# A two-layer diffusion trunk on one core: the opening takes the key and value product block by block, and tiles get sizes in multiples of 512 bytes

## The chip, the core and the metric

The kernel runs on one core of a Trainium2 chip. Its engines work side by side, each on a queue of its own that it takes strictly in order: TensorE (PE) multiplies, VectorE (DVE) and ScalarE (ACT) work on elements, GpSimd (POOL) helps, and SyncE (SP) issues most transfers from DRAM. Engines wait for each other by semaphores. The metric is the device time of one execution in microseconds (us), and less is better.

## What is computed

Two layers of a token mixer with 512 latent tokens and 256 context tokens of width 1024. Each layer norms and modulates the tokens, projects them with `w_in`, runs attention, a gated MLP with chunks and a convolution beside each other, merges them by gates, and adds a squared-ReLU MLP.

```python
mod  = (jax.nn.silu(c) @ ada_w[l] + ada_b[l])[:, None, :]
sh1, sc1, g1, sh2, sc2, g2 = jnp.split(mod, 6, axis=-1)
h  = modulate(rms_norm(x,  mix_pre_g[l]), sh1,  sc1)      # 512 latent tokens
hc = modulate(rms_norm(xc, mix_pre_g[l]), shc1, scc1)     # 256 context tokens
p  = h @ w_in[l]
q    = apply_rope(q_heads(p, q_norm_g[l]), cos, sin)
k, v = kv_heads(p[..., K_OFF:GU_OFF], k_norm_g[l])
...
attn = latent_attention(q, jnp.concatenate([kc, k], 1), jnp.concatenate([vc, v], 1))
y = mixer_merge(p, attn, ...)       # attention, gMLP and convolution branches, gates, w_out
x = x + g1 * rms_norm(y, mix_post_g[l])
x = x + g2 * rms_norm(sq_relu_mlp(modulate(rms_norm(x, ffn_pre_g[l]), sh2, sc2), w1, w2), ffn_post_g[l])
```

## The kernel before, in words

Products are done in three passes. Each fp32 operand is split into a high and a low part (`whi`, `wlo` for weights, two tiles of `hT`, `hB`, `z` or `gin` for data), and PE multiplies high by high, high by low and low by high. A weight arrives by a transfer of 512 KB into a raw tile (`wraw`, two buffers, and `xraw`, as many as a stage asks for); ScalarE casts it to `whi` (L171), and VectorE or GpSimd subtracts to get `wlo` (L174).

A layer runs through stages: attention, gMLP with the convolution (`gmlp_conv`), `conv_out`, and the MLP. Ahead of the first layer stands the stage `start` (L1045 on). It loads X (six blocks of 128 tokens: X0 to X3 latent, X4 and X5 context), norms them, turns them with PE (`transposed`, L403) into columns `xT`, which ScalarE and VectorE copy out of PSUM in turns (L1066, L1068), gets shift and scale of the first layer in four blocks (`ada_shift_scale(j)`, L303 to L324, each from four transfers of 512 KB of `ada_w`), and modulates and splits the columns into `hT` (`modulated`, L1071 on). Block j of shift and scale serves the column tiles 2j and 2j+1. In `ada_shift_scale` PE leaves sums in four bands of partitions; they are copied to `adrow` (L313), turned by four transposes (L316), and added up by VectorE (L318 to L324).

The key and value weights are four raw loads of 512 KB (`wload_kv`, here kv0 to kv3). The product itself is in `attention` (`keys_values`, L532): 8 column tiles, 6 token blocks, 3 passes, so 144 matmuls of 512 columns, in three PSUM tiles of two banks each (`ps`, three buffers). Other PSUM tiles are single banks (`pq`, two buffers).

In `conv_out`, `across` (L955 on) spreads a value per token over all partitions: for each block of 128 tokens VectorE puts the values on a diagonal (`dg`), and PE multiplies it with a constant (L961); the result is copied to `bc` (L963), with which the eight `yr` tiles are scaled (L1006), activated (L1007) and split into `z` for the product with `w_conv_o`.

No order is written out by hand. The program is put into queues by a scheduler that models the engines' time and picks instructions by it; what the source fixes is which operations there are, in which tiles and with how many buffers, since an instruction that needs a buffer waits for its last reader.

Of the kernel before, what the change touches and what calls it, by code (L numbers as in the profile page):

```python
# [11 lines left out]
F32 = mybir.dt.float32  # L12
# [28 lines left out]
JOINT_DOWN = [1, 0]  # L41
EPS = 1e-6
# [12 lines left out]
def trunk_kernel(ctx: ExitStack, tc: tile.TileContext, x, c, ctx_in, c_ctx, ada_w, ada_b, mix_pre_g, mix_post_g,  # L55
# [4 lines left out]
    cst = ctx.enter_context(tc.tile_pool(name="cst", bufs=1))  # L60
    outer = ctx.enter_context(tc.tile_pool(name="outer", bufs=1))
# [33 lines left out]

    def o_(shape, tag, bufs, dt=F32):
        return outer.tile(shape, dt, tag=tag, bufs=bufs, name=nm(tag))

    def t_(shape, tag, bufs, dt=F32):
        return stage_pool[0].tile(shape, dt, tag=tag, bufs=bufs, name=nm(tag))  # L100

    ident = cst.tile([P, P], F32, name="ident")
# [8 lines left out]
    for r in range(2):  # L111
        nc.gpsimd.memset(pick[:, r, r:r + 1], 1.0)

# [142 lines left out]
    def parameters():  # L256
        rows = t_([P, 2, P], "rows", 1)
        nc.sync.dma_start(rows[0:96, 1, :], ada_b.rearrange("l (t p) -> (l t) p", p=P))
        yield
        for i, src in enumerate((mix_pre_g, mix_post_g, gmlp_norm_g, conv_b, conv_norm_g, conv_norm_b,  # L260
                                 ffn_pre_g, ffn_post_g)):
            nc.sync.dma_start(rows[16 * i:16 * i + 16, 0, :], src.rearrange("l (t p) -> (l t) p", p=P))
            if i < 6:
                yield
# [4 lines left out]
        nc.tensor.transpose(pv[:, 0:P], rows[:, 0, :], ident)  # L269
        nc.tensor.transpose(pv[:, P:P + 100], rows[0:100, 1, :], ident[:100, :100])  # L270
# [25 lines left out]
    def ada_shift_scale(j):  # L296
# [965 lines left out]
```

## Time and profile before

| | |
|---|---|
| median of 3 runs | 2648.12 us (2647.98 to 2650.31) |
| profiled execution, whole | 2647.3 us |
| its span | 2645.5 us |
| PE busy | 2591.1 us, 98% of the span |
| DVE, ACT, POOL busy | 63%, 41%, 16% |
| PE busy in the first 20 us | 6.31 us |

The span is the stretch that the profile covers, from the first to the last instruction; the profiled execution has 1.8 us around it. Matmuls overlap, so their listed durations (0.39 us for 512 columns) are longer than the distance from one start to the next (0.23 us), and the distance is what counts. An idle stretch is read with what ended it: `<-DMA x` is a transfer that landed, `<-ACT x` a result of ScalarE.

### The profile page before, as it was taken

What the parts mean: (1) busy time and instruction counts of PE and PEld (TensorE: products, weight loads), DVE (VectorE), ACT (ScalarE), POOL (GpSimd) and SP (SyncE); (2) the same over time, 40 slices, a digit from 0 to 9 for tenths busy, and PEclk for the clock granted to TensorE, in tenths of its full rate; (3) what the DMA queues carried; (4) which work ended last, traced back from release to release, by engine and by line L of the source; (5) the groups of instructions that cost most, each with busy time, mean ns of one, the idle gap of its engine ahead of it and who ended that gap; (6) DMA issues with size and microseconds to landing.
All of it is one profiled execution on the core that took longest, in us unless ns stands there. A gap on an engine that the chain in (4) does not pass through costs nothing.

```text
span 2645.5 us, 37736 instructions
## 1 busy us (share of the span) xinstructions
PE 2591.1 (98%) x15133; PEld 2266.0 (86%) x15133; DVE 1658.5 (63%) x2663; ACT 1076.2 (41%) x1848; POOL 435.0 (16%) x310
## 2 busy tenths in 40 slices
PE   7999999999999999999999999999999999999998
PEld 5989988888888899888888899888888888988888
DVE  5746847489864648445564478777679855734436
ACT  4646434344134636322131355554343244633324
POOL 0000015466463200000000000000465510000000
PEclk9999999999999999999999999999999999999999
DMA  7211134233345345243464342112433455533233
GB/s 250 63 43 37 36 107 137 62 99 95 104 130 173 102 165 154 76 130 120 127 199 129 121 151 88 57 41 72 124 108 100 138 159 173 155 112 96 96 101 106
DMA packets 322241, 300.13 MB, mean 113 GB/s; under 512 B 11517, under 2 KB 268817, under 8 KB 322065
## 3 DMA queue, kind: packets, MB, share of 16 engines
q1 hardware_dynamic: 309360, 271.20, 33.2%
q10 hardware_dynamic: 12704, 26.51, 2.8%
q8 instruction: 119, 1.95, 0.3%
q14 instruction: 58, 0.47, 0.1%
HBM read 275.63 MB, written 22.04 MB: 113 GB/s over the span
## 4 chain that ended last, share of the span: by engine, by line
PE 92%; DVE 3%; DMA 2%; ACT 2%; issue 1%; SPq 0%; DVEq 0%; ACTq 0%
PE ps L192 44%; PE ps L494 16%; PE ps L206 9%; PE pq L192 8%; PE pq L206 4%; PE pq L669 3%; PE ps L635 2%; PE ps L658 1%; PE ps L532 1%; DVE wlo L174 1%; ACT whi L171 1%; PE ps L919 1%; PE pq L403 0%; PE ps L574 0%; DMA xraw<-in_ada_w_dram 0%
## 5 line engine op out<-in xcount | busy, mean ns | idle before, releaser
L192 PE MATMUL ps<-hB,whi 128*128 128x512 f32 (+1 forms) x2272 | 591.9, 359 | 5.0 <-DVE ff L1175 2.3
L171 ACT CAST whi<-wraw 128x1024 fp32r<-128x1024 f32 x261 | 273.8, 1050 | 638.8 <-PE ps L192 315.9
L174 POOL TENSOR_TENSOR wlo<-wraw,whi 128x1024 fp32r<-128x1024 f32 x96 | 230.7, 2404 | 1549.2 <-ACT whi L171 1533.5
L192 PEld LDWEIGHTS ps<-hB,whi 128*128 128x128 f32 x2272 | 387.6, 188 | 71.3 <-DVE ff L1175 2.7
L837 DVE SCALAR_TENSOR_TENSOR cy<-G,cw,cy 128x768 f32<-128x768 f32 (+1 forms) x464 | 404.3, 888 | 11.5
L192 PE MATMUL ps<-hB,wlo 128*128 128x512 f32 (+1 forms) x1136 | 371.9, 357 | 0.0
L494 PE MATMUL ps<-whi,hT 128*128 128x512 f32 x1152 | 356.7, 389 | 0.6 <-ACT whi L171 0.6
L174 DVE TENSOR_TENSOR wlo<-wraw,whi 128x1024 fp32r<-128x1024 f32 x165 | 204.7, 1241 | 201.1 <-ACT whi L171 196.8
L192 PE MATMUL ps<-hT,whi 128*128 128x512 f32 (+1 forms) x1408 | 318.7, 344 | 0.6 <-ACT gu L915 0.6
L494 PEld LDWEIGHTS ps<-whi,hT 128*128 128x128 f32 x1152 | 216.2, 188 | 46.4 <-ACT whi L171 1.1
L192 PEld LDWEIGHTS ps<-hT,whi 128*128 128x128 f32 x1408 | 221.1, 189 | 34.3 <-ACT gu L915 1.1
L174 DVE TENSOR_TENSOR wlo<-xraw,whi 128x1024 fp32r<-128x1024 f32 x109 | 133.3, 1223 | 185.0 <-ACT whi L171 184.5
L206 PE MATMUL ps<-whi,hT 128*128 128x256 f32 x1280 | 232.0, 283 | 0.0
L192 PEld LDWEIGHTS ps<-hB,wlo 128*128 128x128 f32 x1136 | 199.4, 188 | 31.6
L494 PE MATMUL ps<-wlo,hT 128*128 128x512 f32 x576 | 224.4, 390 | 0.0
L171 ACT CAST whi<-xraw 128x1024 fp32r<-128x1024 f32 x109 | 114.2, 1049 | 258.9 <-PE ps L494 118.9
L206 PEld LDWEIGHTS ps<-whi,hT 128*128 128x128 f32 x1280 | 199.6, 192 | 0.5 <-issue 0.4
L192 PE MATMUL ps<-hT,wlo 128*128 128x512 f32 x704 | 190.2, 343 | 0.0
L206 PE MATMUL ps<-wlo,hT 128*128 128x256 f32 x640 | 181.2, 284 | 0.6 <-DVE wlo L174 0.6
L343 POOL TENSOR_TENSOR asum<-asum,aprod 128x512 f32<-128x512 f32 x84 | 111.6, 1329 | 105.7 <-ACT aprod L341 63.2
L494 PEld LDWEIGHTS ps<-wlo,hT 128*128 128x128 f32 x576 | 108.1, 188 | 22.6 <-issue 0.4
L192 PEld LDWEIGHTS ps<-hT,wlo 128*128 128x128 f32 x704 | 110.2, 189 | 16.0
(299 smaller groups left out, 4315.1 us busy)
## 6 DMA issues: line engine op xcount, KB each, us to landing
wraw<-in_w_in_dram SPq DMA_DIRECT2D x134, 512.0 KB, 3.7
xraw<-in_w_ff_dram SPq DMA_DIRECT2D x89, 512.0 KB, 3.9
wraw<-in_w_ff_dram SPq DMA_DIRECT2D x63, 512.0 KB, 3.9
xraw<-in_ada_w_dram SPq DMA_DIRECT2D x39, 512.0 KB, 5.2
wraw<-in_ada_w_dram SPq DMA_DIRECT2D x33, 512.0 KB, 4.2
araw<-in_ada_w_dram SPq DMA_DIRECT2D x48, 256.0 KB, 2.9
xraw<-in_w_out_dram SPq DMA_DIRECT2D x18, 512.0 KB, 8.3
wraw<-in_w_attn_o_dram SPq DMA_DIRECT2D x16, 512.0 KB, 3.5
```

The costliest lines, as they stand in the source:

```text
L171: nc.scalar.copy(hi, raw)
L174: e.tensor_tensor(lo, raw, hi.bitcast(F32), ALU.subtract)
L192: nc.tensor.matmul(ps[:, d0:d0 + n], wt[:, k, c0:c0 + P], xt[:, s0:s0 + n], start=k == 0 and j == 0, stop=k == nk - 1 and j == 2)
L206: nc.tensor.matmul(o, xt[:, tok0:tok0 + P], wt, start=k == 0 and j == 0, stop=k == nk - 1 and j == 2)
L343: nc.gpsimd.tensor_tensor(sums[r], sums[r], t, ALU.add)
L494: nc.tensor.matmul(o, xt[:, tok], wt[:, k, :], start=kt == k == j == 0, stop=kt == 3 and k == 1 and j == 2)
L532: nc.tensor.matmul(o, xt[:, tok], wt, start=k == 0 and j == 0, stop=k == KB - 1 and j == 2)
L635: nc.tensor.matmul(ps[:, s0 - key0:s0 - key0 + n], a[:, i * P:(i + 1) * P], b[:, s0:s0 + n], start=m == 0, stop=m == 2)
L658: nc.tensor.transpose(pt[:, kt * P:(kt + 1) * P], Pm[:, kt * P:(kt + 1) * P], ident)
L669: nc.tensor.matmul(po[:, :256], a[:, kt0 + kt, vs], b[:, kt, :], start=kt == 0 and m == 0, stop=kt == nkt - 1 and m == 2)
L837: nc.vector.scalar_tensor_tensor(done if t == TAPS - 1 else y, G[:, :, t:t + 256], cw[:, t * 8 + cidx:t * 8 + cidx + 1], y, op0=ALU.mult, ...
L919: nc.tensor.matmul(ps[:, n * P:(n + 1) * P], gv[cidx // 4][:, n, (cidx % 4) * P:(cidx % 4 + 1) * P], wsT[:, g, :], start=True, stop=True)
```

## The change

**The opening.** The key and value product moves from `attention` into the stage `start`, into the function `kv_step` (L1110). For each block j its four column-tile halves are multiplied as soon as they are modulated, latent tokens first and context tokens behind them, and between them stand the passes of the next block of shift and scale. `pe()` keeps these PE instructions in the order of the program; the other engines' queues are still put together by the scheduler. The raw key and value loads get `xraw` tiles of their own (10 instead of 6). X0 to X3 are loaded first, then ada 0, ten small rows, kv0, X4 and X5, and then ada j and kv j in turns. The row `ada_b` is issued by ScalarE. Norms are taken for pairs of blocks, the context transposes go through single banks. In `ada_shift_scale` the four transposes become four matmuls with `every`, a constant of two columns that adds the bands, and VectorE has two operations instead of five.

**Memory.** `tile_in` pads every tile of at least 512 bytes a partition to a multiple of 512; smaller ones go to a pool `tiny` with a filler in front. `dg` goes from one buffer per token block to 2, `junkg` shares the tile `gt`, `gb` shares `rt2`.

On SP this is the queue around the small rows, before and then after. In it X are token blocks, rows are the small parameter rows, and in_w_in loads of 128x2x512 are kv0 and so on.

```order
L262 DMA rows_129<-in_ffn_post_g_dram 16x128
L265 DMA rows_129<-in_q_norm_g_dram 2x128
L266 DMA rows_129<-in_k_norm_g_dram 2x128
L1043 DMA X_104<-in_ctx_dram 128x1024
L1043 DMA X_105<-in_ctx_dram 128x1024
L169 DMA wraw_151<-in_w_in_dram 128x2x512
L169 DMA wraw_157<-in_w_in_dram 128x2x512
L303 DMA xraw_163<-in_ada_w_dram 128x4x256
```

```order
L327 DMA xraw_147<-in_ada_w_dram 128x4x256
L288 DMA rows_135<-in_mix_pre_g_dram 16x128
...
L289 DMA rows_135<-in_q_norm_g_dram 2x128
L290 DMA rows_135<-in_k_norm_g_dram 2x128
L1095 DMA xraw_159<-in_w_in_dram 128x2x512
L1058 DMA X_111<-in_ctx_dram 128x1024
L1058 DMA X_112<-in_ctx_dram 128x1024
L327 DMA xraw_295<-in_ada_w_dram 128x4x256
```

The ten small rows stand together between ada 0 and kv0, where they stood between the X blocks; the context blocks come behind kv0. In both queues an entry waits until the transfer eight places ahead has landed.

On ScalarE this is the queue around the copies of X's columns and the casts `whi` of the key and value weights, before and then after (two pieces: kv0's cast, then kv2's).

```order
L394 ACTIVATE xn_111,ss_262<-X_105 128x1024
L171 CAST whi_153<-wraw_151 128x1024
L171 CAST whi_159<-wraw_157 128x1024
L1068 COPY xT_53_207<-ps_198 128x512
L1068 COPY xT_56_220<-ps_211 128x512
L1068 COPY xT_59_233<-ps_224 128x512
L1068 COPY xT_62_246<-ps_237 128x512
L313 COPY adrow_344<-pq_327 128x512
L171 CAST whi_252<-xraw_250 128x1024
L171 CAST whi_258<-xraw_256 128x1024
```

```order
L207 CAST whi_305<-xraw_159 128x1024
L1082 COPY xT_55_227<-ps_218 128x512
L418 ACTIVATE xn_117,ss_327<-X_111 128x1024
L1082 COPY xT_58_240<-ps_231 128x512
L418 ACTIVATE xn_118,ss_327<-X_112 128x1024
L339 COPY adrow_257<-pq_209 128x512
...
L207 CAST whi_540<-xraw_450 128x1024
L207 CAST hT_119<-xT_87_367 128x256
L1082 COPY xT_93_385<-pq_380 128x256
L207 CAST hT_121<-xT_88_369 128x256
L1082 COPY xT_96_394<-pq_389 128x256
L339 COPY adrow_421<-pq_404 128x512
```

The squares of the context blocks moved behind kv0's cast, between the copies, and kv2's cast came to stand ahead of the last copies of the context columns.

On PE this is `across` in the first layer's `conv_out`, before and then after; hT by whi and wlo is the gate product that runs behind or around it.

```order
L192 MATMUL ps_8390<-hT_126,wlo_8388 128x256
L961 MATMUL ps_8449<-dg_8450,means 128x128
L961 MATMUL ps_8449<-dg_8453,means 128x128
L961 MATMUL ps_8449<-dg_8456,means 128x128
L961 MATMUL ps_8449<-dg_8459,means 128x128
L961 MATMUL ps_8449<-dg_8462,means 128x128
L961 MATMUL ps_8449<-dg_8465,means 128x128
L192 MATMUL ps_8476<-hT_112,whi_8472 128x512
```

```order
L976 MATMUL ps_8465<-dg_8466,means 128x128
L976 MATMUL ps_8465<-dg_8469,means 128x128
L221 MATMUL ps_8492<-hT_119,whi_8488 128x512
...
L976 MATMUL ps_8465<-dg_8472,means 128x128
L976 MATMUL ps_8465<-dg_8475,means 128x128
L221 MATMUL ps_8492<-hT_126,whi_8488 128x512
...
L976 MATMUL ps_8465<-dg_8478,means 128x128
L976 MATMUL ps_8465<-dg_8481,means 128x128
```

The six matmuls came apart into three pairs, with twenty rows of the gate product, which are ten pairs of 512 and 256 columns, between one pair and the next.

The diff, cut to its core:

```diff
+LINE = 512
+FILL = 24
...
+    def tile_in(pool, shape, tag, bufs, dt, align=LINE):
+
+        size = 2 if dt == BF16 else 4
+        n = math.prod(shape[1:])
+        whole = -(-n * size // align) * align // size
+        if whole == n:
+            return pool.tile(shape, dt, tag=tag, bufs=bufs, name=nm(tag))
+        t = pool.tile([shape[0], whole], dt, tag=tag, bufs=bufs, name=nm(tag))[:, :n]
+        return t if len(shape) == 2 else t.rearrange("p (a b) -> p a b", b=shape[2])
...
+    def small_tile(shape, dt=F32):
+        return math.prod(shape[1:]) * (2 if dt == BF16 else 4) < LINE
+
     def o_(shape, tag, bufs, dt=F32):
-        return outer.tile(shape, dt, tag=tag, bufs=bufs, name=nm(tag))
+        if small_tile(shape, dt):
+            return tiny.tile(shape, dt, tag=tag, bufs=bufs, name=nm(tag))
+        return tile_in(outer, shape, tag, bufs, dt)
...
+    nc.gpsimd.memset(tiny.tile([P, FILL], F32, name="fill"), 0.0)
...
+    every = cst.tile([P, 2], F32, name="every")
+    nc.vector.tensor_reduce(every, ident.rearrange("p (q s) -> p s q", q=4)[:, 0:2, :], axis=AX.X, op=ALU.add)
...
+    def pe(ins):
+
+        return tc.keep_in_program_order(ins) if in_order[0] else ins
...
-        nc.sync.dma_start(rows[0:96, 1, :], ada_b.rearrange("l (t p) -> (l t) p", p=P))
+        nc.scalar.dma_start(rows[0:96, 1, :], ada_b.rearrange("l (t p) -> (l t) p", p=P))
...
         rows = t_([P, 512], "adrow", 2)
         nc.scalar.copy(rows, pa)
+        yield
         pt = ps1()
         for t in range(4):
-            nc.tensor.transpose(pt[:, t * P:(t + 1) * P], rows[:, t * P:(t + 1) * P], ident)
+            pe(nc.tensor.matmul(pt[:, 2 * t:2 * t + 2], rows[:, t * P:(t + 1) * P], every, start=True, stop=True))
         m = mods[0][:, 0:2, 2 * j:2 * j + 2, :]
-        nc.vector.tensor_reduce(m, pt.rearrange("p (v t q s) -> p v t s q", v=2, t=2, q=4)[:, :, :, 0:2, :],
-                                axis=AX.X, op=ALU.add)
-        ab = vecs[0]["adab"][:, 0:16].rearrange("p (v k) -> p v k", v=2)[:, :, 2 * j:2 * j + 2]
-        for r in range(2):
-            nc.vector.tensor_tensor(m[:, :, :, r], m[:, :, :, r], ab, ALU.add)
-        for r in range(2):
-            nc.vector.scalar_tensor_tensor(m[:, 1, :, r], m[:, 1, :, r], 1.0, vecs[0]["pre"][:, 2 * j:2 * j + 2],
-                                           op0=ALU.add, op1=ALU.mult)
+        ab = vecs[0]["adab"][:, 0:16].rearrange("p (v k o) -> p v k o", v=2, o=1)[:, :, 2 * j:2 * j + 2, :]
+        nc.vector.tensor_tensor(m, pt[:, 0:8].rearrange("p (v t s) -> p v t s", v=2, t=2),
+                                ab.to_broadcast([P, 2, 2, 2]), ALU.add)
+        pre = vecs[0]["pre"][:, 2 * j:2 * j + 2].rearrange("p (k o) -> p k o", o=1)
+        nc.vector.scalar_tensor_tensor(m[:, 1], m[:, 1], 1.0, pre.to_broadcast([P, 2, 2]), op0=ALU.add, op1=ALU.mult)
...
-            gb = t_([P, HD], "gb", 1)
+            gb = t_([P, HD], "rt2", 1)
...
-                junk = t_([P, 512], "junkg", 1, BF16)
+                junk = t_([P, 512], "gt", 1, BF16)
...
-                dg = t_([P, P], "dg", NT)
+                dg = t_([P, P], "dg", 2)
...
-    with stage("start", 6):
+    with stage("start", 10):
...
+        def kv_raw(k):
+            raw = raw_tile([P, 2, 512])
+            nc.sync.dma_start(raw, w_in[0][k * 256:(k + 1) * 256, K0:K0 + 512].rearrange("(k p) c -> p k c", p=P))
+            return raw
...
+        def kv_step(grp, k):
+            xhi, xlo = hT[k]
+            whi, wlo = (w[:, k % 2, :] for w in w_kv[k // 2])
+            for i in range(grp[0], grp[0] + grp[1]):
+                o = kv_ps[i // 2][:, (i % 2) * 512:(i % 2) * 512 + 512]
+                tok = slice(i * P, (i + 1) * P)
+                for n, (xt, wt) in enumerate(((xhi, whi), (xhi, wlo), (xlo, whi))):
+                    pe(nc.tensor.matmul(o, xt[:, tok], wt, start=k == 0 and n == 0, stop=k == KB - 1 and n == 2))
+
+        next(small)
+        x_load(0, X[0:4], 0, nc.sync)
+        ada = [ada_shift_scale(j) for j in range(4)]
+        next(ada[0])
+        next(small)
+        raws = [kv_raw(0)]
+        x_load(0, X[4:6], 4, nc.sync)
+        in_order[0] = True
+        for i in (0, 2):
+            normed(X, xn, (i, 2, 0))
+        next(ada[0])
+        x_columns(LAT, (0, 4))
         for _ in small:
             pass
         next(ada[0])
+        x_columns(LAT, (4, 8))
+        next(ada[0])
+        kv_ps = [ps2() for _ in range(3)]
+        w_kv = []
         for j in range(4):
+            ks = (2 * j, 2 * j + 1)
             if j < 3:
                 next(ada[j + 1])
+                raws.append(kv_raw(j + 1))
+            w_kv.append(kv_parts(raws[j]))
+            for k in ks:
+                modulated(LAT, k)
+            if j:
+                for k in ks:
+                    modulated(CTXG, k)
+            kv_step(LAT, ks[0])
+            if j == 0:
+                normed(X, xn, CTXG)
+                kv_step(LAT, ks[1])
+                x_columns(CTXG, (0, 8))
+                for k in ks:
+                    modulated(CTXG, k)
+            if j < 3:
+                next(ada[j + 1])
+                next(ada[j + 1])
+            if j:
+                kv_step(LAT, ks[1])
+            else:
+                kv_step(CTXG, ks[0])
+            if j < 3:
+                next(ada[j + 1])
+            if j:
+                kv_step(CTXG, ks[0])
+            kv_step(CTXG, ks[1])
+        in_order[0] = False
         late_parameters()
```

Of the opening the diff shows the new lines only; the old ones are in the listing above.

## Rows read from the trace of the kernel before

**Rows 1.** page: busy times, then groups, xcount | us, mean ns

```profile
PE 2591.1 (98%) x15133; PEld 2266.0 (86%) x15133; DVE 1658.5 (63%) x2663; ACT 1076.2 (41%) x1848; POOL 435.0 (16%) x310
...
L192 PE MATMUL ps<-hB,whi 128*128 128x512 f32 (+1 forms) x2272 | 591.9, 359 | 5.0 <-DVE ff L1175 2.3
...
L192 PE MATMUL ps<-hT,whi 128*128 128x512 f32 (+1 forms) x1408 | 318.7, 344 | 0.6 <-ACT gu L915 0.6
```

**Rows 2.** windows: busy us (instructions) by engine, PEclk, DMA share, GB/s

```profile
0.00:20.00 20.00, 6.31 (x31) 5.12 (x35) 7.49 (x21) 12.49 (x19) 1.28 (x12) 1.00 0.85 285
20.00:40.00 20.00, 17.52 (x133) 11.31 (x132) 12.93 (x36) 7.56 (x14) 0.00 (x0) 1.00 1.08 387
```

**Rows 3.** timeline, K/V product: start us, us, engine line op, idle before

```profile
28.71 0.50 PE L532 MATMUL ps<-whi,hT 128*128 128x512 f32 x1 [0.73 <-ACT hT L178]
...
70.06 0.39 PE L532 MATMUL ps<-whi,hT 128*128 128x512 f32 x1
70.29 0.28 PE L206 MATMUL pq<-whi,hT 128*128 128x256 f32 x1
```

**Rows 4.** groups, 28.7 to 70.29, PE: xcount | us, mean | idle

```profile
L532 PE MATMUL ps<-whi,hT 128*128 128x512 f32 x96 | 30.9, 398 | 1.0 <-ACT hT L178 0.7 <-DVE hT L179 0.2
```

**Rows 5.** timeline, ScalarE in the opening

```profile
4.54 1.06 ACT L394 ACTIVATE xn<-X 128x1024 f32<-128x1024 f32 x1 [1.57 <-DMA X<-in_x_dram]
...
16.57 1.04 ACT L171 CAST whi<-wraw 128x1024 fp32r<-128x1024 f32 x1
...
50.88 1.05 ACT L171 CAST whi<-wraw 128x1024 fp32r<-128x1024 f32 x1 [0.83 <-DMA wraw<-in_w_in_dram]
```

**Rows 6.** timeline, SP's queue, the first reads of ada

```profile
11.07 5.08 SPq L303 DMA_DIRECT2D xraw<-in_ada_w_dram  x4
```

**Rows 7.** page, DMA issues: xcount, KB each, median us to landing

```profile
xraw<-in_w_ff_dram SPq DMA_DIRECT2D x89, 512.0 KB, 3.9
wraw<-in_w_ff_dram SPq DMA_DIRECT2D x63, 512.0 KB, 3.9
```

**Rows 8.** groups by shape, 0 to 75, ScalarE and VectorE

```profile
L174 DVE TENSOR_TENSOR wlo<-wraw,whi 128x1024 fp32r<-128x1024 f32 x6 | 7.3, 1225 | 3.5 <-ACT whi L171 3.3
...
L178 ACT CAST hT<-xT 128x512 fp32r<-128x512 f32 x8 | 4.7, 619 | 12.6 <-DVE xT L1076 12.6
...
L1076 DVE TENSOR_SCALAR xT<-xT,mod 128x512 f32<-128x512 f32 x8 | 4.1, 544 | 0.0
...
L1066 DVE COPY xT<-ps 128x512 f32<-128x512 f32 x4 | 2.7, 686 | 0.0
...
L313 ACT COPY adrow<-pq 128x512 f32<-128x512 f32 x4 | 2.3, 581 | 4.8 <-PE pq L310 4.8
```

**Rows 9.** timeline, conv_out of the first layer

```profile
876.91 1.50 PE L961 MATMUL ps<-dg,means 128*128 128x128 f32 x12
...
878.45 0.80 ACT L963 COPY bc<-ps 128x768 f32<-128x768 f32 x1
...
896.09 0.86 PE L192 MATMUL ps<-z,whi 128*128 128x512 f32 x4
...
898.95 1.56 ACT L178 CAST z<-yr 128x768 fp32r<-128x768 f32 x2
```

**Rows 10.** timeline, PE: start of a block with hT and the next

```profile
652.08 0.74 PE L192 MATMUL ps<-hT,whi 128*128 128x512 f32 x3
...
660.40 0.74 PE L192 MATMUL ps<-gin,whi 128*128 128x512 f32 x3
...
728.77 0.74 PE L192 MATMUL ps<-hT,whi 128*128 128x512 f32 x3
...
737.25 0.74 PE L192 MATMUL ps<-hT,whi 128*128 128x512 f32 x3
```

**Rows 11.** waits of PE, 163.9 to 167.5: us, times, longest

```profile
PE ps L658 <- DVE PT L662: 2.5, 1, 2.5
```

**Rows 12.** windows, after that wait

```profile
167.00:171.00 4.00, 3.92 (x16) 3.26 (x17) 2.72 (x7) 1.82 (x4) 0.00 (x0) 0.57 0.43 125
```

More of the change, by code (lines that the diff above doesn't have):

```diff
@@ L60, in trunk_kernel @@
     cst = ctx.enter_context(tc.tile_pool(name="cst", bufs=1))
+    tiny = ctx.enter_context(tc.tile_pool(name="tiny", bufs=1))
     outer = ctx.enter_context(tc.tile_pool(name="outer", bufs=1))
@@ L498, in streamed, with attention @@
                 tick(kt)
[L501 removed]
+    def attention(l, hT, T, last, md, kv_ps=None):
         NT = T // P
@@ L520, in rope_tabs, with keys_values @@
             return C, S
-        def keys_values(ws):
-            pss = [ps2() for _ in range(3)]
-            for k in range(KB):
-                xhi, xlo = hT[k]
-                whi, wlo = (w[:, k % 2, :] for w in ws[k // 2])
-                for i in range(6):
-                    o = pss[i // 2][:, (i % 2) * 512:(i % 2) * 512 + 512]
-                    tok = slice(i * P, (i + 1) * P)
-                    for j, (xt, wt) in enumerate(((xhi, whi), (xhi, wlo), (xlo, whi))):
-                        nc.tensor.matmul(o, xt[:, tok], wt, start=k == 0 and j == 0, stop=k == KB - 1 and j == 2)
+        def keys_values(pss):
             k_nat = t_([P, 6, 256], "PT", 4)
@@ L605, in attention @@
         vlo = t_([P, 6, 256], "vlo", 1, F32R)
-        if w_kv is not None:
-            k_nat = keys_values(w_kv)
+        if kv_ps is not None:
+            k_nat = keys_values(kv_ps)
         else:
@@ L1051, in trunk_kernel, with x_columns @@
         xT = {}
-        def x_columns(grp):
-            normed(X, xn, grp)
+        def x_columns(grp, kbs):
             w = grp[1] * P
-            per = 1024 // w
-            for kb in range(0, KB, per):
-                ps = ps2()
+            new, per = (ps2, 1024 // w) if grp == LAT else (ps1, 512 // w)
+            for kb in range(kbs[0], kbs[1], per):
+                ps = new()
                 for q in range(per):
@@ L1077, in modulated, with kv_parts @@
             split(hT[k][0][:, s], hT[k][1][:, s], t)
-        for i in range(6):
-            x_load(0, X[i:i + 1], i, nc.sync)
-            for _ in range(2):
-                next(small, None)
+        def kv_raw(k):
+            raw = raw_tile([P, 2, 512])
+            nc.sync.dma_start(raw, w_in[0][k * 256:(k + 1) * 256, K0:K0 + 512].rearrange("(k p) c -> p k c", p=P))
+            return raw
+        def kv_parts(raw):
+            hi, lo = (o_([P, 2, 512], tag, 4, F32R) for tag in ("whi", "wlo"))
+            split(hi, lo, raw)
+            return hi, lo
@@ L1083, in trunk_kernel @@
+        x_load(0, X[0:4], 0, nc.sync)
[9 more added lines that the diff above has]
+        x_columns(LAT, (0, 4))
         for _ in small:
             pass
-        w_kv = wload_kv(0, False, (0, 1))
-        ada = [ada_shift_scale(j) for j in range(4)]
         next(ada[0])
-        x_columns(LAT)
```

32 lines of the change are left out of this document (13 added, 19 removed).

## The prediction

> **What bounds the kernel now.** I read the busy times first. TensorE (PE) is busy 2591.1 us of the 2645.5 us span [rows 1], so a change gains only by taking passes off PE, by shortening them, or by closing the few stretches where PE waits. The table by stage shows where those are: in the first 20 us PE is busy 6.31 us, in the next 20 us 17.52, while DMA moves 285 and then 387 GB/s at a share above 1 [rows 2]. The opening therefore waits for data. The timeline gives the edges: the first matmul of the K/V product (L532) starts at 28.71, the last at 70.06, and the query product (L206) follows at 70.29, 0.23 later, as one 512-column matmul follows another [rows 3]. In these 41.6 us PE waited some 1.0 us in all before the product's matmuls [rows 4]; after it PE is the bound. What the opening can give is thus the time before 28.71 and no more; what it can lose is any hole it opens afterwards.
>
> **Opening, start of the product.** The changed order takes X0 to X3 and the four blocks of ada 0 first: 8 transfers of 512 KB. At 387 GB/s one takes 1.36 us; the first X had landed at 4.54 [rows 5], so the eighth lands at 4.5 + 7 x 1.36 = 14. ada 0 is so there early; in before the first reads of ada were issued from 11.07 on [rows 6]. But then ten small rows stand ahead of kv0 in SP's queue, and each entry waits for the one eight places ahead to have landed. The eighth small row thus waits until 14; two more and kv0 follow at some 0.45 each, so kv0 is issued at 15.5 and lands about 4 us later (512 KB of weights took a median 3.9 [rows 7]): 19.5. The ctx blocks land at 20.9 and 22.2. In before kv0's cast began at 16.57, after both ctx blocks [rows 5].
>
> Both engines that evacuate work in their queues' order. On ScalarE kv0's cast stands ahead of the first copy of the transposed X, and the squares of both ctx blocks ahead of the adrow copy. From 22.2: square (1.06 [rows 5]) with its read-out 1.25, adrow 0.58, the `every` passes and their hand-over: 24.6. VectorE has eight small steps of the ctx norm, about 0.2 each, and two copies at 0.69 between 23.5 and the scales: 26.4. Then two scale steps 0.4, two modulations 0.54 each, of which the second runs beside the first cast of 0.62 [rows 8]: the product starts at about **28.0, 0.7 earlier** than 28.71. Four us of earlier ada data are lost behind kv0 and the ctx blocks.
>
> **Opening, holes behind the start.** The ctx transposes now lie behind the start: 16 of 128 columns at about 0.11 (an estimate, half of the 0.23 of 512 columns at the least) = 1.7, and 8 adaLN passes 0.5; 12 full transposes become tiny passes, -1.0. Net **+1.2**. Then three holes, all of one kind, a cast that waits for a DMA ahead of work that PE needs:
> (a) kv2 is the 21st transfer of 512 KB. 4.5 + 20 x 1.36 + about 3 for the hole that the small rows tear = 35 to 36 (DMA is at its limit from 20 to 40 [rows 2]). Its cast (1.04 [rows 5]) and its subtraction (1.22 [rows 8]) stand ahead of the last ctx copies; those are done at 36 + 1.1 + 1.2 + 0.7 = 39.0. ada 1 needs the bank that they free. PE has from 28.0 on 24 matmuls at 0.23 = 5.5, the transposes 1.7, and some 1.4 of waits of these on the ctx norm and on banks: dry at 36.6. Hole **2.4**.
> (b) The last two blocks of ada 3 and kv3 need buffers that ada 1's passes free, so they are issued after 39, and kv3 lands at 39.8 + 3.9 = 43.7. Its cast stands ahead of the casts of hT for block 1: 43.7 + 1.05 + 0.62 = 45.4. PE ends ada 1 and the 12 ctx matmuls at 39.0 + 2.3 + 2.7 = 44.0. Hole **1.3**, and 0.7 for the subtraction.
> (c) The first query weights, which ScalarE cast at 50.88 in before, after a wait of 0.83 on their DMA [rows 5], now stand ahead of block 2's scales on VectorE and land about 54.6: cast, subtraction, scales and modulations end at 58.5, PE is dry at 56.8. Hole **1.7**, and 0.4.
> Sum of the opening: -0.7 + 1.2 + 6.5 - 1.0 (the old holes) = +6; with the landing times 1 us later each hole grows by that. I take **+7**, bounds +4 and +11.
>
> **conv_out.** `dg` gets 2 buffers instead of one per token block. Before, 6 matmuls (12 passes) run in 1.50 us from 876.91, `bc` is copied at 878.45, and the product with z starts at 896.09 [rows 9]. Now passes and VectorE take turns inside a gate product: the third pair stands 20 pairs of matmuls later in PE's queue, 20 x 0.347 = 6.9 us. From `bc` to the last z ScalarE has 0.80 + 1.28 + 8 x 1.02 + 8 x 0.82 = 16.8 of work and took 878.45 to 898.95 + 1.56 = 900.5, 22 us [rows 9]; so 5 us of other work can go ahead, and the last z comes 2 to 7 us later. PE needs it at 896.09 + 7 x 1.04 = 903.4, and its cast was done at 900.5: slack 2.9. Cost 0 to 4, I take **+2.5**. Layer 1 has 4 blocks and the later start is covered: 0 to 1. `junkg` and `gb` move into tiles that are used elsewhere in time; ScalarE (41% busy [rows 1]) hides that, 0 to 1 without cover.
>
> **Addresses.** Tiles become multiples of 512 bytes in size. In the built kernel every fp32r operand then starts 192 bytes past a multiple of 512; before, hT, whi and wlo started at 256, hB at 0, z at 64, gin at 224. The trace shows two paces: a block of 24 pairs (512 and 256 columns) takes 8.32 us with hT from 652.08 on and 8.48 with hT from 728.77 on [rows 10]. One address shows both, so the address alone doesn't set the pace, and it is worth 0.16 us a block. The page has 1408 and 2272 matmuls of this gemm with whi, and half as many again with wlo [rows 1]: 5520, of which at most 2400 pairs = 100 blocks. With half of them slow now, all fast or all slow is -8 or +8. I take **0**, with -8 and +8 for the range.
>
> Transfers land at these addresses too. `xraw` outside the opening started at 96 past 512 bytes and `wraw` at 256, and both take 3.9 us to land from w_ff [rows 7], so a start off 256 costs nothing that shows. The Trainium skill ("DMA: Bandwidth & Descriptors", How a descriptor splits into AXI transactions) says that a descriptor which does not begin at a multiple of 256 bytes pays for an extra transaction. By my estimate from its table a row of 1 KB would cost 38 beats for 32, and the opening's 36 us of transfers 6 us more; by the trace it is 0.
>
> **Clock.** PE waits once for 2.5 us between 163.9 and 167.5 [rows 11]; from 167 to 171 the granted clock is 0.57 [rows 12]: (1 - 0.57) x 4 / 0.5 = 3.4 of them at the 1.2 GHz level, the rest at 2.4. Hole (a) may do the same: half speed for 3.4 us costs 1.7. I take **+1.5** for this and a part of a second fall, bounds 0 and 5.
>
> **Sum.** 7 + 2.5 + 0 + 1.5 = +11. The profiled execution took 2647.3 us, 0.8 below the median of the runs, 2648.1. Forecast 2648.1 + 11 = **2659**.
>
> **Rivals.**
> B, the opening goes as it is written: kv0 lands before the copies need it, the product starts near 24 and no cast waits. -4.7 + 1.2 = -3.5, conv_out +2.5: 2647, no difference. For it: VectorE and ScalarE are far from full (12.93 and 7.56 of 20 [rows 2]). Against: the order of the queues, which is fixed in the build.
> C, as forecast and dearer: all blocks at the slow pace (+8), or each hole drops the clock (+5 and more): 2667 to 2680. For it: about half the blocks run at the slow pace already, and hole (a) is as long as the wait that was followed by a fall. By the Trainium skill's rule of transactions, above, the time would be 2659 + 6 = 2665; the equal landing times speak against it, and of C's chance it has 0.03.
> D, faster: B together with all blocks at the fast pace, 2648.1 - 3.5 + 2.5 - 8 = 2639. It decides once the pace saves over 5 us and no hole is over 1 us. For it: moving and stationary operand now lie alike in all products. Against: it needs two things of which the rows show neither.
> E, the change doesn't do what it says: the addresses are not multiples of 512 and the product doesn't start earlier. That is part of A and C.
>
> **How the numbers follow.** Forecast A (2653 to 2667) 0.58, C 0.13, B 0.16, D 0.13. The measurement can tell about 0.2% from no change, 5.3 us: 2642.8 to 2653.4. Slower: C and nearly all of A, 0.69. Same: B and the tail of A, 0.18. Faster: D, 0.13. The range leaves out most of C and D: 2643 to 2670; A alone is 2651 to 2667.
>
> **What will show it.** Start of the first matmul of L1110 (28.0; 24 would be B) and of the query product after it (77); waits of 2.4, 1.3 and 1.7 us behind casts `whi` of kv2, kv3 and the first query weights; kv0's cast at 19.5; the wait before the z product; granted clock around 37 to 42; pace of the hT blocks in the gate products, 8.32 or 8.48. Wrong would be a product that starts before 26, no waits after it, or a time that moves evenly over all stages.

## The result, and the profile after

The changed kernel takes 2670.64 us (median of 4 runs, 2665.78 to 2673.3), the kernel before 2649.22 beside it. The ratio is 1.0076 with a 95% interval of 1.006 to 1.0092, so it is slower by 20 us (16 to 24). The forecast, 2659, had the direction and about half of the size. The median lies 0.6 us beyond the upper end of its range (2670); by the ratio, on the 2648.1 us from which it was made, the time is 2668 and inside.

The page of the changed kernel, busy times; PE has 10.5 us more of them than in [rows 1], and the span is 18.5 us longer (2664.0):

```profile
PE 2601.6 (98%) x15149; PEld 2271.8 (85%) x15149; DVE 1662.5 (62%) x2664; ACT 1075.0 (40%) x1848; POOL 435.8 (16%) x311
```

The first two stages, to be read against [rows 2]: busy us of PE, PEld, DVE, ACT and POOL, then the granted clock, the share of DMA and GB/s.

```profile
0.00:20.00 20.00, 8.76 (x55) 5.17 (x56) 6.82 (x29) 7.39 (x12) 1.34 (x13) 1.00 0.80 265
20.00:40.00 20.00, 14.35 (x63) 11.56 (x60) 12.61 (x32) 10.01 (x19) 0.00 (x0) 0.74 1.08 360
```

PE has more to do in the first 20 us (8.76 for 6.31), since ada 0 is there early, and less in the next 20 (14.35 for 17.52). Two numbers there were not in the forecast: the mean granted clock is 0.74 where it was 1.00 (the forecast had its fall later, behind the hole ahead of ada 1), and the transfers run at 360 GB/s where they ran at 387, at the same share of 1.08.

The timeline of PE, rows with a wait in front of them, and the first query product (columns as in [rows 3]):

```profile
27.93 0.79 PE L1110 MATMUL ps<-whi,hT 128*128 128x512 f32 x1 [1.70 <-ACT hT L207]
...
35.74 1.03 PE L427 MATMUL pq<-ident,xn 128*128 128x128 f32 x8
37.26 1.31 PE L427 MATMUL pq<-ident,xn 128*128 128x128 f32 x8 [0.49 <-DVE xT L1080]
41.23 1.93 PE L334 MATMUL pq<-xraw,c 128*32 128x256 f32 x32 [2.66 <-DVE xT L1080]
...
48.47 0.50 PE L1110 MATMUL ps<-whi,hT 128*128 128x512 f32 x1 [1.47 <-ACT hT L207]
...
49.81 1.22 PE L1110 MATMUL ps<-whi,hT 128*128 128x512 f32 x2 [0.61 <-DVE hT L208]
...
63.12 0.50 PE L1110 MATMUL ps<-whi,hT 128*128 128x512 f32 x1 [0.66 <-ACT hT L207]
...
64.17 0.74 PE L1110 MATMUL ps<-whi,hT 128*128 128x512 f32 x2 [0.32 <-DVE hT L208]
...
83.75 0.28 PE L235 MATMUL pq<-whi,hT 128*128 128x256 f32 x1
```

The product starts at 27.93, 0.8 earlier than in [rows 3], and the query product follows at 83.75 instead of 70.29: the opening costs 13.5 us. ScalarE's queue names what PE waits for; these are the casts of kv0, kv2, kv3 and of the first query weights, each with the wait for its transfer (as in [rows 5]):

```profile
19.73 1.05 ACT L207 CAST whi<-xraw 128x1024 fp32r<-128x1024 f32 x1 [8.98 <-DMA xraw<-in_w_in_dram]
...
38.20 1.04 ACT L207 CAST whi<-xraw 128x1024 fp32r<-128x1024 f32 x1 [1.02 <-DMA xraw<-in_w_in_dram]
...
46.85 1.04 ACT L207 CAST whi<-xraw 128x1024 fp32r<-128x1024 f32 x1 [3.04 <-DMA xraw<-in_w_in_dram]
...
59.26 1.05 ACT L200 CAST whi<-wraw 128x1024 fp32r<-128x1024 f32 x1 [2.73 <-DMA wraw<-in_w_in_dram]
```

kv2's cast at 38.20, with its subtraction on VectorE, stands ahead of the copies that PE waits for until 41.23. kv3's at 46.85 stands ahead of the cast of hT that PE waits for until 48.47. The subtraction of the query weights, cast at 59.26, stands on VectorE ahead of the scales for 63.12.

### The profile page after: what moved, and what is told of

Read it like the earlier page. It is cut to its first block, busy times and chain, and to the rows that moved or that the text cites. A ratio compares the mean times of both kernels' runs of the same rounds, so it can differ in the third digit from the quotient of the medians.

```text
span 2664.0 us, 37776 instructions
## 1 busy us (share of the span) xinstructions
PE 2601.6 (98%) x15149; PEld 2271.8 (85%) x15149; DVE 1662.5 (62%) x2664; ACT 1075.0 (40%) x1848; POOL 435.8 (16%) x311
## 4 chain that ended last, share of the span: by engine, by line
PE 90%; DVE 3%; DMA 3%; ACT 2%; issue 1%; SPq 0%; DVEq 0%; ACTq 0%
PE ps L221 44%; PE ps L518 16%; PE ps L235 9%; PE pq L221 8%; PE pq L235 4%; PE pq L684 3%; PE ps L650 2%; PE ps L673 1%; PE ps L1110 1%; DMA xraw<-in_w_in_dram 1%; DVE wlo L203 1%; ACT whi L200 1%; DMA xraw<-in_ada_w_dram 1%; PE ps L934 1%; PE pq L427 0%
## 5 line engine op out<-in xcount | busy, mean ns | idle before, releaser
L518 PEld LDWEIGHTS ps<-wlo,hT 128*128 128x128 f32 x576 | 108.1, 188 | 22.6 <-issue 0.4
L235 PEld LDWEIGHTS ps<-wlo,hT 128*128 128x128 f32 x640 | 123.4, 193 | 1.2 <-DVE wlo L203 1.1
```

Source lines behind the costliest of these rows:

```text
L235: nc.tensor.matmul(o, xt[:, tok0:tok0 + P], wt, start=k == 0 and j == 0, stop=k == nk - 1 and j == 2)
L518: nc.tensor.matmul(o, xt[:, tok], wt[:, k, :], start=kt == k == j == 0, stop=kt == 3 and k == 1 and j == 2)
```

## What the opening is made of

From the starts of PE's passes between the first matmul of the product and the query product, after against before: the 144 matmuls take 42.0 us instead of 33.9 (+8.1), the context transposes with the waits between and behind them (0.49 and 2.66) 5.5 (there were none behind the start), the adaLN passes 5.6 for 6.0 (-0.4), the passes that turn `adrow` 2.4 for 1.5 (+0.9), the `crows` transposes +0.1. That is +14.2, less 0.8 for the earlier start, 13.5. Of the +8.1, waits are 3.1 (rows 48.47 to 64.17 above; before had 0.2), and the granted clock is about 4:

```profile
20.00:26.00 6.00, 3.97 (x23) 3.63 (x20) 4.69 (x13) 5.28 (x10) 0.00 (x0) 0.71 1.07 370
26.00:28.00 2.00, 0.30 (x3) 0.21 (x2) 1.97 (x10) 0.74 (x2) 0.00 (x0) 0.50 1.09 358
...
50.00:52.00 2.00, 2.00 (x5) 1.61 (x6) 1.03 (x3) 0.00 (x0) 0.00 (x0) 0.50 0.01 3
```

At 0.50 the engine runs at the 1.2 GHz level. 16 matmuls of the product start 0.43 us apart instead of 0.23, between 28.5 and 32.8 and between 50.4 and 53.0: 16 x 0.20 = 3.2, with the edges about 4.

The first fall came ahead of the product. A mean of 0.71 from 20 to 26 and 0.50 from 26 on put it at 22.5, and it lasted until 32.7. At 22.5 PE stood in a wait:

```profile
22.69 1.97 PE L427 MATMUL ps<-ident,xn 128*128 128x128 f32 x8 [2.03 <-DVE xT L1080]
```

These transposes waited for a copy of X's columns that VectorE took at 21.95, behind the subtraction of kv0, whose cast had come at 19.73. So this wait is one more of the same kind, ahead of the start. The second fall came at 49.8, behind the waits that ended at 48.47 and 49.81 (1.47 and 0.61 us, with two matmuls in between), and lasted until 53.2.

## The experiments

The theory after the result: the new opening loses by casts that wait for a transfer at a place in their queue where work for PE stands behind them, and by the clock that falls behind such waits; `dg` costs 2 to 3 us in conv_out; and raw tiles that start off a multiple of 256 bytes are filled more slowly. Rivals: the addresses cost on PE too and carry most of the loss; the new order of loads by itself slows the transfers; the ada transfers are the bound, so that holes only move. Differences are against the kernel before on the same chip, from the ratio and 2648.7 us.

**e1, e2, e3: addresses, opening, memory.** e1 is the changed kernel with

```diff
-FILL = 24
+FILL = 40
```

> The changed kernel with 64 bytes more of filler, so that every padded tile starts 256 bytes past a multiple of 512 instead of 192; the queues are the same row by row. Queue theory (the loss is casts that wait for a DMA ahead of work that PE needs, and the lower clock behind it): as the changed kernel, +17 to +22 us over before, transfers at 350 to 365 GB/s between 26 and 38 us, kv2's cast at 38, query product at 83 to 84. Address theory (starts that are not multiples of 256 slow the transfers and the operands): transfers at 385 GB/s as before, kv2's cast at 36.5, query product at 81 or earlier, total +10 to +15.

Measured 1.0069 (1.0052 to 1.0086), +18.3 us, which can't be told from the changed kernel's 20. e2 has the new opening and nothing of the memory part:

```diff
-    with stage("start", 6):
+    with stage("start", 10):
...
+                    pe(nc.tensor.matmul(o, xt[:, tok], wt, start=k == 0 and n == 0, stop=k == KB - 1 and n == 2))
```

> The new opening alone: tiles, pools, dg, junkg and gb as before. Queue theory: query product at 83 to 84 instead of 70.3, with the holes of 2.7, 1.5 and 0.7 us and two stretches at half clock; the rest of the kernel as before, so +13 to +15 us. Address theory: the opening loses at most half of that, +5 to +8, and transfers run at 385 GB/s.

Measured 1.006 (1.0045 to 1.0075), +15.9; the query product starts at 83.12. e3 has the memory part and the opening of before:

```diff
+LINE = 512
+FILL = 24
...
-                dg = t_([P, P], "dg", NT)
+                dg = t_([P, P], "dg", 2)
```

> The new memory alone: sizes in multiples of 512 bytes, the tiny pool with its filler, dg with 2 buffers, junkg and gb in shared tiles; the opening as before. The padded tiles start 160 bytes past a multiple of 512. Queue theory: opening as before (query product at 70.3), conv_out of the first layer loses 2 to 3 us, the second under 1, total +2 to +5. Address theory: the transfers of the opening fall below 370 GB/s and the query product comes 2 us later or more, total +6 to +10.

Measured 1.0017 (1.0008 to 1.0027), +4.5; the query product starts at 71.17. The two halves add up: 15.9 + 4.5 = 20.4 for 20. So the opening is four fifths of the loss, and in e2 it loses all of it without the new sizes of tiles (its raw tiles start off 256 too, at 32, see below). In e1 the queues are those of the changed kernel, and yet the opening is 2.3 us shorter:

```profile
27.21 0.80 PE L1110 MATMUL ps<-whi,hT 128*128 128x512 f32 x1 [2.52 <-ACT hT L207]
...
34.12 1.04 PE L427 MATMUL pq<-ident,xn 128*128 128x128 f32 x8
...
38.95 1.93 PE L334 MATMUL pq<-xraw,c 128*32 128x256 f32 x32 [2.00 <-DVE xT L1080]
...
46.78 0.50 PE L1110 MATMUL ps<-whi,hT 128*128 128x512 f32 x1 [2.02 <-ACT hT L207]
...
81.48 0.28 PE L235 MATMUL pq<-whi,hT 128*128 128x256 f32 x1
```

Of the 2.3, 0.7 are the earlier start and 0.7 the shorter wait ahead of ada 1 (2.00 for 2.66). The other 0.9 are a shorter first fall of the clock (26.7 to 30.1): from the first matmul of the product to the first context transpose e1 takes 34.12 - 27.21 = 6.9 us, the changed kernel 7.8. The transfers say why the casts come earlier. One line for 26 to 38 us each, of the kernel before, the changed one, and e1:

```profile
26.00:38.00 12.00, 10.92 (x74) 7.11 (x73) 7.54 (x18) 4.64 (x10) 0.00 (x0) 1.00 1.09 383
```

```profile
26.00:38.00 12.00, 9.81 (x39) 7.60 (x39) 7.02 (x19) 2.93 (x5) 0.00 (x0) 0.72 1.08 357
```

```profile
26.00:38.00 12.00, 9.25 (x40) 7.17 (x40) 7.38 (x15) 5.01 (x10) 0.00 (x0) 0.86 1.08 386
```

Raw tiles that start on a multiple of 256 bytes (0 and 256 in before, 256 in e1) are filled at 383 and 386 GB/s; at 192 (after) it is 357, at the same share of busy DMA engines. In e2 (32) it is 356. The order of the loads is not the cause: it is the same in e1 and after, and e9 shows the lower rate with the old one.

**e9: the address alone.** The kernel before with

```diff
+    nc.gpsimd.memset(cst.tile([P, 40], F32, name="fill"), 0.0)
```

> The kernel before with 160 bytes of filler ahead of all tiles and nothing else: X and the raw tiles of the opening start 160 bytes past a multiple of 256, the raw tiles of the later stages, which were 96 past, start on one. Address theory, after the first four runs: the transfers of the opening fall from 385 to about 350 GB/s and the query product comes 1 to 2 us later, the rest within 2 us: +0 to +3. Rival (the new order of loads slowed the transfers): 385 GB/s and no difference.

```profile
26.00:38.00 12.00, 10.30 (x72) 6.70 (x71) 7.75 (x19) 4.83 (x11) 0.00 (x0) 1.00 1.10 348
```

348 GB/s instead of 383, with the old order of loads. In this opening it costs 1.0 us (query product at 71.31), and in all 1.0005 (0.9996 to 1.0015), which can't be told from no change. The rival on the order of loads falls. (The total mixes two things: the raw tiles of the later stages moved onto a multiple of 256 by the same edit.) A slow fill costs 1.0 us in the old opening, and in the new one, where casts wait for it, up to the 2.3 of e1.

**e4: dg.** The kernel before with

```diff
-                dg = t_([P, P], "dg", NT)
+                dg = t_([P, P], "dg", 2)
```

> The kernel before with one edit: dg has 2 buffers. If the spread pairs of the diagonal product make the product with z wait: +2 to +4 us, all of it between 876 and 917 us and a little near 2190. If ScalarE and VectorE catch up: within 0.5 us of before.

Measured 1.0011 (1.0001 to 1.002), +2.9. In its trace the distance to before grows from 1.7 us at the first dg pass to 3.8 at the end of the first block of the z product, so 2.1 us in the first layer; in the second layer's conv_out, around 2190, it grows by 0.4. The changed kernel shows the chain (against [rows 9]):

```profile
888.63 0.61 PE L976 MATMUL ps<-dg,means 128*128 128x128 f32 x4
...
892.54 0.61 PE L976 MATMUL ps<-dg,means 128*128 128x128 f32 x4
...
896.46 0.61 PE L976 MATMUL ps<-dg,means 128*128 128x128 f32 x4
...
897.10 0.80 ACT L978 COPY bc<-ps 128x768 f32<-128x768 f32 x1 [6.88 <-PE ps L976]
...
911.40 1.62 PE L221 MATMUL ps<-z,whi 128*128 128x512 f32 x6 [1.14 <-ACT z L207]
```

The pairs stand 3.9 us apart, `bc` comes 8.5 us behind the first pass instead of 1.5, and the z product starts, then runs dry and waits 1.14 us for a cast of z.

**e5, e6: the small rows and the order of kv.** e5 is e1 with a small row behind each big transfer:

```diff
-        next(small)
-        x_load(0, X[0:4], 0, nc.sync)
+        for i in range(4):
+            x_load(0, X[i:i + 1], i, nc.sync)
+            next(small)
...
+                if j == 0:
+                    next(small)
```

> The kernel of e1 with the ten small rows issued one behind each big transfer instead of all ten between ada 0 and kv0. Queue theory: kv0 lands at 16 instead of 19, the product starts near 25 instead of 27.2, and all later transfers come 2 to 3 us earlier, so the holes keep their place in the order but move with them: total 2 to 3 us less than e1, +14 to +16 over before. Rival (PE and its order bound the product, what is gained at the start is lost in longer holes): within 1 us of e1.

Measured 1.0054 (1.0037 to 1.0071), +14.3, 4 less than e1, though the intervals overlap. It has no trace that can be read; e13 shows the start with the rows spread. e6 loads kv1 to kv3 ahead of ada 1 in addition:

```diff
         x_load(0, X[5:6], 5, nc.sync)
+        raws += [kv_raw(k) for k in (1, 2, 3)]
...
-                raws.append(kv_raw(j + 1))
```

> The kernel of e5 with kv1, kv2 and kv3 loaded right behind the context blocks, ahead of ada 1. No cast of key and value weights waits any more when work for PE stands behind it, but ada 1 to 3 come 4 us later. Theory of the holes: the holes behind kv2 and kv3 (2.0 and 2.0 us in e1) go, total 2 to 4 us less than e5, +11 to +13. Rival (the ada transfers are the bound, the holes only move to the passes of ada): no less than e5.

Measured 1.0062 (1.0047 to 1.0077), +16.4: a miss. The opening did get shorter, the query product starts at 78.04 instead of 81.48 in e1, but the start did not move as meant:

```profile
26.68 0.79 PE L1117 MATMUL ps<-whi,hT 128*128 128x512 f32 x1 [3.49 <-ACT hT L208]
...
29.50 1.22 PE L1117 MATMUL ps<-whi,hT 128*128 128x512 f32 x2 [1.60 <-DVE hT L209]
...
39.34 1.93 PE L340 MATMUL pq<-xraw,c 128*32 128x256 f32 x32 [0.33 <-DVE xT L1087]
...
45.34 0.50 PE L1117 MATMUL ps<-whi,hT 128*128 128x512 f32 x1 [0.18 <-ACT hT L208]
...
78.04 0.28 PE L236 MATMUL pq<-whi,hT 128*128 128x256 f32 x1
```

The holes behind kv2 and kv3 are gone (0.33 and 0.18 for 2.00 and 2.02 in e1), so the casts were their cause and ada was not; e8 shows it again. With the second hole the second fall of the clock is gone too. But the three casts and subtractions, which no longer wait, now come before the start: PE waits 3.49 us ahead of the product and 1.60 behind its first matmuls. And the total doesn't show the 3.4 us at all; what happened to them is told under e17.

**e8, e17: the clock.** Both get 16 transposes more, whose result nobody reads, ahead of the product:

```diff
+        busy = ps1()
+        for _ in range(16):
+            pe(nc.tensor.transpose(busy[:, 0:P], xn[0][:, 0:P], ident))
         kv_ps = [ps2() for _ in range(3)]
```

> The kernel of e1 with 16 transposes more on PE, whose result nobody reads, just ahead of the product; by the way the scheduler puts the casts of kv2 and kv3 behind the last copies of the context columns. Theory of clock and holes: PE is busy through the wait ahead of the product, the granted clock is 1.00 from 27 on (in e1 0.73 between 28 and 32), which gives back 1 to 2 us, and the two holes of 2.0 us go, so +12 to +14 over before. Rival (the clock is set by something else and PE is bound by ada): clock as in e1, total +16 to +18.

> The kernel of e6 with 16 transposes more on PE ahead of the product, whose result nobody reads; VectorE's and ScalarE's queues are row by row the same. Clock theory: the 3.5 us wait ahead of the product is filled, the granted clock between 28 and 32 is 1.00 instead of 0.50, the query product comes 2 us earlier than 78.0, total 2 us less than e6. Rival (the clock follows something else, or the waits behind take it back): 0.50 again, no difference.

e8 (on e1) measured 1.0032 (1.0019 to 1.0045), +8.5, ten us less than e1; six of them are the opening's, whose query product starts at 75.46. The scheduler also put kv2's and kv3's casts four rows further back, behind the copies and the casts of hT that PE needs. Its waits, and its clock from 28 to 32:

```profile
27.23 0.50 PE L1110 MATMUL ps<-whi,hT 128*128 128x512 f32 x1 [0.72 <-ACT hT L207]
...
33.12 1.03 PE L427 MATMUL pq<-ident,xn 128*128 128x128 f32 x8
...
36.28 1.93 PE L334 MATMUL pq<-xraw,c 128*32 128x256 f32 x32 [0.33 <-DVE xT L1080]
...
42.28 0.50 PE L1110 MATMUL ps<-whi,hT 128*128 128x512 f32 x1 [0.18 <-ACT hT L207]
```

```profile
28.00:32.00 4.00, 4.00 (x18) 3.27 (x19) 3.01 (x4) 1.05 (x1) 0.00 (x0) 1.00 1.08 381
```

The clock stays at 1.00, and the holes are 0.33 and 0.18 instead of 2.00 and 2.02: the same loads in the same order, with the casts a few rows later. Two causes went at once, but the starts price them apart. From the first matmul of the product to the first context transpose, where the casts of kv2 and kv3 have no part, e8 takes 33.12 - 27.23 = 5.9 us and e1 6.9, so the first fall of the clock cost e1 1.0. The two holes are 3.5, and e1's second fall (47.2 to 50.6 in its trace, behind the second hole) is most of the remaining 1.5.

e17 was to price the clock alone, since it is e6 with the same queues on VectorE and ScalarE in the opening. Measured 1.0046 (1.003 to 1.0061), +12.2; the windows of e6 and then its own, 28 to 32 and 32 to 36, and its waits:

```profile
28.00:32.00 4.00, 2.50 (x6) 2.02 (x7) 3.69 (x8) 0.00 (x0) 0.00 (x0) 0.50 1.09 382
32.00:36.00 4.00, 4.00 (x17) 3.22 (x17) 0.00 (x0) 0.00 (x0) 0.00 (x0) 0.90 1.09 381
```

```profile
28.00:32.00 4.00, 2.41 (x8) 1.96 (x9) 3.78 (x8) 0.00 (x0) 0.00 (x0) 0.84 1.09 382
32.00:36.00 4.00, 4.00 (x15) 3.20 (x14) 0.00 (x0) 0.00 (x0) 0.00 (x0) 0.74 1.09 385
```

```profile
26.77 0.50 PE L1117 MATMUL ps<-whi,hT 128*128 128x512 f32 x1 [1.50 <-ACT hT L208]
...
29.59 0.72 PE L1117 MATMUL ps<-whi,hT 128*128 128x512 f32 x2 [2.09 <-DVE hT L209]
...
78.14 0.28 PE L236 MATMUL pq<-whi,hT 128*128 128x256 f32 x1
```

The expectation failed: the query product starts at 78.14, as in e6. The transposes kept the clock up to the start of the product, but then a fall came behind the wait of 2.09 us after its first matmuls (1.60 in e6): at 30.7 instead of 26.0, so 0.84 and 0.74 instead of 0.50 and 0.90. Here filling one wait moved the fall to the next; in e8 and e13, whose longest wait behind the start is 0.5, none comes in the opening. The four us by which e17's median lies below e6's (the intervals overlap) lie behind the opening; the first dg pass of e6, then of e17:

```profile
888.34 0.61 PE L982 MATMUL ps<-dg,means 128*128 128x128 f32 x4
```

```profile
883.55 0.60 PE L982 MATMUL ps<-dg,means 128*128 128x128 f32 x4
```

From the query product to the first dg pass e6 takes 888.34 - 78.04 = 810.3 us, e17 805.4, with the same starts of the tiles and queues that differ in a dozen rows. e1 takes 808.6 and e8 807.2, again at 256; the changed kernel takes 804.9 at 192, the kernel before 806.6. So these stretches differ by 5 us between single traces, from more than one chip, at one and the same layout, and no address is seen to set it.

Part of it is the clock. From 170 to 185 the granted clock is 0.89 in e6 and 1.00 in e17, which is at most 0.11 x 15 = 1.7 of the 4.9 us. Between the changed kernel and e1, whose queues are the same, it can be most of the 3.7: 1.00 for 0.96 from 160 to 200 and 0.98 for 0.96 from 600 to 680, so 1.6 + 1.6 us. What else sets the pace is open. That is also why the totals of e5 and e6 don't follow their openings, as far as e6's trace tells.

**e10: aligned, without the dg edit.** e3 with another filler, and one dg slice per block:

```diff
-FILL = 24
+FILL = 48
...
-                dg = t_([P, P], "dg", 2)
+            dgs = t_([P, T], "z", 16)
...
+                dg = dgs[:, i * P:(i + 1) * P]
```

> The kernel before with the padded tiles and the tiny pool, all padded tiles 256 bytes past a multiple of 512, but with one dg slice per token block (slices of a z tile), so that the spread pairs are gone; the opening as before. It is e3 with another filler and without the dg edit. Address theory (only starts off 256 cost): opening at 385 GB/s, query product at 70.3 to 70.7, the rest as before or up to 3 us faster where z, gin and attn stood off 256: -2 to +1. If padding by itself costs or gives: outside of that.

Measured 1.0008 (0.9999 to 1.0016), +2.1, which can't be told from no change; the query product starts at 70.74. The median lies just above the expected +1, its interval reaches down into that range. No gain by starts at one multiple for all operands shows.

**e13: all repairs together.** The changed kernel with e1's filler, e5's rows, e8's transposes and e10's dg.

> All repairs of the changed kernel together: starts at 256, small rows one by one behind the big transfers, 16 transposes more ahead of the product, one dg slice per token block. If the causes add up as told: start of the product 25, query product at 72 to 73, conv_out as before, total +2 to +4 over before, so still no gain. If an unknown part of the change costs or gives elsewhere: +7 or more, or below 0.

Measured 1.0016 (1.0007 to 1.0026), +4.2.

```profile
25.72 0.50 PE L1118 MATMUL ps<-whi,hT 128*128 128x512 f32 x1 [0.31 <-ACT hT L208]
...
34.73 1.93 PE L340 MATMUL pq<-xraw,c 128*32 128x256 f32 x32 [0.33 <-DVE xT L1088]
...
73.88 0.28 PE L236 MATMUL pq<-whi,hT 128*128 128x256 f32 x1
```

The product starts 3 us earlier than in before, and the query product still 3.6 us later: 48.2 us lie between them instead of 41.6. By the starts, the context transposes without their waits are 2.4 of the 6.6, the passes with `every` 0.9, the waits 1.9 (2.1 for 0.2 in before), the adaLN passes -0.4, and some 1.7 lie between matmuls of the product, mostly where it resumes behind other passes or a wait (0.34 us from the first start to the second instead of 0.23). So the causes add up nearly as told, and no version here beats the kernel before.

## Why the forecast was right, and where it was off

- **What bounds the kernel**: right. What is lost in the opening is not given back (13.5 us at the query product, 11.7 of it still there at the first dg pass, 888.63 for 876.91).
- **Start of the product**: right to 0.1. kv0's cast came at 19.73 (19.5), the product at 27.93 (28.0). e13 shows the rows' share: with them spread the start is 25.72, for 27.21 in e1. Not in the forecast: kv0's cast also made PE wait 2.03 us ahead of the start, in which the clock fell.
- **Holes**: the mechanism right, and e6 and e8 show it; (a) was 2.66 (2.4), (b) 1.47 and 0.61 (1.3 and 0.7), (c) 0.66 and 0.32 (1.7 and 0.4). That (a) has its size is in part luck: kv2's cast and the copies behind it came 2.2 us later than forecast (38.20 and 41.2 for 36 and 39.0), and PE ran dry 2.0 later (38.6 for 36.6), since the slow clock had cost it 1.9 (7.8 us to the first context transpose for 5.9 in e8). So the query product came at 83.75, and not at 77.
- **Two slips in the sum**: I took off 1.0 for the old holes, but 0.73 of it stand ahead of the product's first matmul [rows 3] and are in the earlier start already; 0.24 were left. And the 1.4 of waits and gaps among the context transposes stood in the time at which PE runs dry, but not in the sum; 1.1 was measured.
- **12 transposes that become tiny passes**: the wrong sign. I put -1.0 for them. 24 passes come in place of 12 (a plain fp32 product takes two each), with 128 weight columns as before and 2 moving columns, and such a pass costs what one with 128 does (0.11 us from start to start within a row of them, for both):

```profile
L343 PE MATMUL pq<-every,adrow 128*128 128x2 f32 x24 | 2.8, 240 | 0.0
```

```profile
L316 PE MATMUL pq<-ident,adrow 128*128 128x128 f32 x12 | 1.8, 272 | 0.0
```

 2.8 us busy for 1.8; by starts, with what follows, 2.4 for 1.5. The term was +0.9.
- **Transfers at starts off 256 bytes**: wrong. I read from [rows 7] that 96 and 256 land alike and took 0. That row is a median over stages in which the DMA engines are mostly far from full (0.1 to 0.5 busy on the page of the changed kernel), and there the rate doesn't show; in the opening, where the DMA engines are full, it is 357 for 383 GB/s. e1 prices it at 2.3 us of the opening, 0.9 of them by way of the clock. The rule of the Trainium skill that I had set aside ("DMA: Bandwidth & Descriptors", How a descriptor splits into AXI transactions) had the direction right; the size by my estimate from its table was 38 beats for 32, 19%, and the runs show 7 to 10%. The same estimate gives 33 beats for a start at 32 and 37 at 160, while the runs show 356 and 348 GB/s beside 357 at 192, so its order is not borne out.
- **Clock**: too small and in another place. I took 1.5 behind hole (a). It fell twice in the opening, at 22.5 in the wait ahead of the start and at 49.8 behind hole (b), for about 4 us of the product; behind (a) it did not fall. A stretch in the first MLP and one near the end have falls too, which the same places of before don't show in its trace:

```profile
1050.00:1066.00 16.00, 14.05 (x64) 11.44 (x62) 12.51 (x31) 9.02 (x23) 0.00 (x0) 0.89 0.36 98
2255.00:2268.00 13.00, 11.36 (x80) 10.96 (x80) 8.04 (x11) 7.48 (x18) 0.00 (x0) 0.87 1.06 375
```

 Of the 18.5 us in the traces 13.9 are there at the end of the first layer's product with z. Of the 4.6 behind it these two falls can be 0.11 x 16 = 1.8 and 0.13 x 13 = 1.7. They need not come from the change: e9, with the old opening, has the first of them too (0.96 from 1030 to 1070, as in the changed kernel; before 1.00). The rest stays open.
- **conv_out**: right, 2.1 in e4 and 2.2 in the changed kernel (2.5).
- **Operand addresses on PE**: right, as far as the runs show: e9 and e10 move all operands, and neither can be told from no change. Both paces are there again: between 640 and 880 the changed kernel has blocks of 8.32 and of 8.48 us. The +-8 us was a spread of the runs, not of the addresses, and 5 of it was seen.
- **Sum**: the opening 13.5 for 7 + 1.5; conv_out 2.2, and in the second layer 0.4 at most (e4); the rest as told under the clock. The term that was mis-sized most is the clock with 2.5, then the tiny passes with 1.9 and the transfers with 1.4 (2.3 less the 0.9 of the clock).

- **Rivals**: B and D fell with the start at 27.93 and three holes behind it. The time lies above the main forecast A (2653 to 2667) and in C's range (2667 to 2680), which had 0.13. Of C's two reasons one holds in part: the clock cost about 4 us in the opening and up to 3.5 later, though not behind every hole. The other, all blocks at the slow pace, does not. So A had the mechanism of the opening, and that the range took in the time is owed to the part of it that was kept for C.

## What to carry over

Before loads are moved, write down for each engine's queue what stands behind each instruction that waits for a transfer: a cast that waits there costs what PE needs behind it, however idle the engine is on average. An earlier start of the bound engine is worth nothing if it is paid with holes, and a hole may cost a second time by the clock, even one ahead of that start. Price a transfer in the stage in which the DMA engines are full, not by a median over all.

## What the runs showed of the hardware

- Transfers into tiles that start off a multiple of 256 bytes run slower where DMA is full: 348 GB/s at 160, 357 at 192, 356 at 32, against 383 to 386 at 0 and 256, at the same share of busy engines.
- A pass of two moving columns (with 128 weight columns) starts 0.11 us behind the one before it, as one of 128 columns does.
- The granted clock fell to 0.50 within a wait of 2.03 us (after, at 22.5) and 1.1 us behind one of 2.09 (e17, at 30.7), in e17 though PE had been filled up to the start of the product. At 0.50 a matmul of 512 columns starts 0.43 us behind the one before it, for 0.23 at 1.00. Behind the wait of 2.66 us that ended at 41.23 the clock did not fall, so the length of the wait alone doesn't decide.
- The passes between the query product and conv_out took 804.9 to 810.3 us in kernels whose operands start alike and in others; falls of the granted clock are a part of the difference (0.89 in e6 and 1.00 in e17 from 170 to 185), the rest is open.
